# One decoder layer on one core: the order of ScalarE, VectorE, loads and TensorE in the up and down projections, from a scheduler's order to a list made in the kernel

## The chip, the core and the metric

The kernel runs on one NeuronCore of a Trainium2 chip. The metric is the time of one execution in microseconds (us) on the device. The kernel before was run three times: 1428.9, 1429.55 and 1432.31 us, so its median is 1429.55 us. One more execution was taken with the hardware profiler; that one took 1434.5 us.

## The reference, cut to what matters

One layer of a hybrid decoder: 256 tokens, width 2048, all in f32. An input projection, a state-space scan beside windowed attention and an output projection come first and are not touched. Then follows the part that the change is about, the feed-forward network, and after it a gated embedding:

```python
u = _rmsnorm(h, ffn_norm_g[i]) @ w_up[i]                    # 2048 -> 2 x 5632
u = _causal_dwconv(u, ffn_conv_w[i], ffn_conv_b[i])         # 3 taps along the tokens
g_ff, u_ff = jnp.split(u, [D_FF], axis=-1)
h = h + (jax.nn.silu(g_ff) * u_ff) @ w_down[i]              # 5632 -> 2048
gate = jax.nn.sigmoid(_rmsnorm(h, ple_norm_g[i]) @ w_ple_gate[i])
pe = _rmsnorm(p[i] @ w_ple_proj[i], ple_post_g[i])
h = h + gate * pe
```

## The kernel before, in words

**Three products for one.** Each f32 factor is split in two parts, a rounded one (names that end in `h`) and the rest (names that end in `l`). A product is three matmuls: high by high, high by low, low by high. So each weight tile `w` (128 x 1024, 512 KB, loaded by SyncE) needs a cast on ScalarE (`wh<-w`, L206) and a subtraction on VectorE (`wl<-w,wh`, L207) before TensorE can use it. "A split" below means this pair. Seven buffers hold raw tiles, and four (a fifth in this stage) hold split ones, so a cast must wait until TensorE has used up the tile that was split five before.

**The stage.** The 5632 columns are worked in 11 pairs of 512 (a chunk of `g` and the same chunk of `u`). For one pair, `up` (L1070) runs eight blocks of 256 rows of the weights. Six are plain: two weight tiles, 24 matmuls each. Two are "mixed" (`MIXED`, blocks 0 and 4; `cell_mixed`, L991): there seven products take the place of eight, on differences of weight quarters, which VectorE forms first (`ta`, `tb`, L997) and which then go through splits of their own; a half tile goes to `vh`, `vl`. A mixed block has 21 matmuls. The eight PSUM banks hold one pair's sums. After the second mixed block, VectorE combines four banks into the staged tiles `c` (L1083 to L1088), and after the last block it adds the other four (L1092).

**The turn.** `gated` (L1050) must turn these four tiles from tokens on partitions to features on partitions: ScalarE copies each into 16-bit halves (`half`, L1041), SyncE issues a DMA transpose (`flip<-half`, L1043), and ScalarE joins the halves (`uc<-flip`, L1044). Then follow the three taps (`cv<-uc`: one pass on ScalarE, two on VectorE, L308 and L310), SiLU, the product and its split into `gh`, `gl`. The taps are put in a list `later`, from which `step` issues one or two behind each block.

**The down projection** (`down`, L1112) takes two pairs at a time (`SEGS`): four output chunks, 48 matmuls each, two of them behind each `up`. Each chunk is added to the residual `h` on VectorE (L418). The first two pairs have no `down` between them, nor is there one between the second and the third.

**The way in.** Four small embedding products (`embed`, L913; their results `c` are copied by VectorE at L918 and stored to `pe_d` by SyncE at L919), the RMS factor `rh` (squares on ScalarE, a power on GpSimd), the scaled residual `cv` (`norm`, L923), and 32 transposes on TensorE with gain and split (`left`, L946; `ah<-b` L209, `al<-b` L210).

**Who sets the order.** On TensorE the order is that of the code (`tc.manual_schedule` with that engine alone). ScalarE, VectorE and SyncE are ordered by the scheduler of the framework, which simulates the program; `high_priority` lifts the squares, `rh`, and the first norms and lefts. PSUM banks come from a pool of eight that goes round. Every engine then works through its own list in order: what stands behind a waiting instruction waits too.

Of the kernel before, what the change touches and what calls it, by code (L numbers as in the profile page):

```python
# [11 lines left out]
F32 = mybir.dt.float32  # L12
F32R = mybir.dt.float32r
# [29 lines left out]
MIXED = (0, 4)  # L43
# [16 lines left out]
def _turns(value):  # L60

    t = value / (2 * PI)
    return _parts(t - round(t), 13, 26)


@with_exitstack
def hybrid_layer(
# [56 lines left out]

    def bank():
        return banks[0].tile([P, NC], F32, tag="b", name=nm("b"))
# [535 lines left out]
    with tc.tile_pool(name="att_s", bufs=2) as as_, tc.tile_pool(name="att", bufs=2, reuse_waits="tile") as ap_, tc.tile_pool(name="ps_sc", bufs=1, space=PSUM) as ps_sc:  # L662
# [224 lines left out]
    by_hand = tc.manual_schedule(engines={PE.engine})  # L887
    by_hand.__enter__()

    with tc.tile_pool(name="ffn", bufs=2, reuse_waits="tile") as fp:  # L890

        def staged(i):
            return sb(fp, [P, NC], f"c{i}", bufs=1)

        more.append(fp)

        class Gated:

            def __init__(self):
                self.t = []  # L900

            def add(self):
                self.t.append([sb(fp, [P, KG, T], f"g{e}", F32R, 3) for e in "hl"])
                return self.t[-1]

            def __call__(self, k, b):
                return [t[:, k % KG, b * P : (b + 1) * P] for t in self.t[k // KG]]

        gT = Gated()
        gT.add()  # L910
        ph, pl = em

        def embed(n):  # L913
            acc = acc_pair()
            gemm(acc, lambda k, b: (ph[:, k, b * P : (b + 1) * P], pl[:, k, b * P : (b + 1) * P]), [w_pe[n, 0]])
            for b in range(NB):
                t = staged(n % 2 * 2 + b)
                V.tensor_copy(t, acc[b])  # L918
                nc.sync.dma_start(pe_d[b, :, n * NC : (n + 1) * NC], t)  # L919

        normed = []

        def norm(n):  # L923
            t = sb(fp, [P, NB, NC], f"cv{n % 2}", bufs=1)
            for b in range(NB):
                hs = hres[b][:, n * NC : (n + 1) * NC]
                if n:
                    S.activation(out=t[:, b, :], in_=hs, func=AF.Copy, scale=rh[:, b : b + 1])
                else:
                    V.tensor_scalar_mul(t[:, b, :], hs, rh[:, b : b + 1])  # L930
            normed.append(t)
# [322 lines left out]
```

## Time and profile before

| | |
|---|---|
| Median of three runs | 1429.55 us |
| The profiled execution, its own time | 1434.5 us |
| Its span, first to last instruction | 1432.6 us |
| TensorE busy | 1413.0 us (99%), 6461 matmuls |
| VectorE busy | 1114.0 us (78%) |
| ScalarE busy | 903.0 us (63%) |
| GpSimd busy | 130.3 us (9%) |
| The stage that the change is about | about 608 to 1343 us of the span |

How to read it: matmuls overlap in the pipeline, so a record of 0.39 us starts every 0.2257 us when nothing holds TensorE up, and the "busy" time covers small delays. A better measure of a delay is the time from one matmul's start to the next, or the number of matmuls in a window of fixed length. TensorE is the engine without slack; the others matter where TensorE waits for them.

### The profile page before, as it was taken

The page shows a single profiled execution, that of the slowest core. Times are in us where ns is not written, and L with a number is a line of the kernel's source. Part 1 is how long each engine was busy: PE and PEld are TensorE (multiplying, and loading weights), DVE is VectorE, ACT ScalarE, POOL GpSimd, SP SyncE. Part 2 cuts the span into 40 slices and gives each one's busy share as a digit, 9 for nine tenths or more (in the row PEclk, how much of TensorE's full clock was granted, in tenths as well). Part 3 has the DMA queues.
Part 4 walks back from the last instruction along what each step waited for, and adds up shares of the span by engine and source line. Part 5 has one row for each costly group of instructions (what it writes and reads, how often), then busy time and mean ns, then how long its engine had stood idle before and what let it go on. Part 6 is the DMA issues. An engine that isn't in the chain of part 4 may idle for free.

```text
span 1432.6 us, 18128 instructions
## 1 busy us (share of the span) xinstructions
PE 1413.0 (99%) x6461; PEld 1154.4 (81%) x6461; DVE 1114.0 (78%) x1480; ACT 903.0 (63%) x1196; POOL 130.3 (9%) x113
## 2 busy tenths in 40 slices
PE   9999999999999999999999999999999999999998
PEld 7888888888777778878787888888888888788887
DVE  7678876776678898698998796878778797877764
ACT  6675555644667757566777476666758576674653
POOL 0002010008344332000000000000000000000000
PEclk9999999999999999999999999999999999999999
DMA  9656656548686878576678777686777777677671
GB/s 348 229 174 197 216 179 189 163 147 231 180 221 186 209 215 219 180 233 199 200 231 194 227 223 204 205 230 204 205 226 196 228 227 207 195 220 213 224 249 64
DMA packets 164906, 296.80 MB, mean 207 GB/s; under 512 B 93200, under 2 KB 96080, under 8 KB 164176
## 3 DMA queue, kind: packets, MB, share of 16 engines
q1 hardware_dynamic: 163952, 292.04, 69.1%
q10 hardware_dynamic: 864, 3.62, 0.7%
q8 instruction: 50, 0.82, 0.2%
q14 instruction: 40, 0.33, 0.1%
HBM read 270.41 MB, written 4.23 MB: 192 GB/s over the span
## 4 chain that ended last, share of the span: by engine, by line
PE 56%; DVE 7%; ACT 3%; DMA 2%; issue 2%; DVEq 0%; ACTq 0%
PE b L987 9%; PE b L988 9%; PE b L986 9%; PE b L244 7%; PE b L242 7%; PE b L243 7%; DVE wl L207 3%; PE acc L242 3%; PE acc L243 2%; PE acc L244 2%; DMA flip<-half 2%; ACT wh L206 1%; DVE cv L310 1%; ACT half L1041 1%; DVE h L418 1%
## 5 line engine op out<-in xcount | busy, mean ns | idle before, releaser
L207 DVE TENSOR_TENSOR wl<-w,wh 128x1024 fp32r<-128x1024 f32 (+1 forms) x473 | 584.0, 1242 | 224.3 <-ACT wh L206 220.7
L206 ACT CAST wh<-w 128x1024 fp32r<-128x1024 f32 (+1 forms) x473 | 490.3, 1045 | 339.3 <-PE b L988 135.9
L987 PE MATMUL b<-wl,ah 128*128 128x512 f32 x484 | 189.3, 391 | 2.8 <-DVE wl L207 2.7
L988 PE MATMUL b<-wh,al 128*128 128x512 f32 x484 | 189.4, 391 | 1.8 <-DVE al L210 1.7
L986 PE MATMUL b<-wh,ah 128*128 128x512 f32 x484 | 189.3, 391 | 1.2 <-ACT wh L206 1.2
L243 PE MATMUL acc<-wl,ah 128*128 128x512 f32 x448 | 176.8, 395 | 1.4 <-DVE wl L207 1.4
L242 PE MATMUL acc<-wh,ah 128*128 128x512 f32 x448 | 176.0, 396 | 0.7 <-DVE h L418 0.6
L244 PE MATMUL acc<-wh,al 128*128 128x512 f32 x448 | 175.6, 392 | 0.0
L242 PE MATMUL b<-wh,gh 128*128 128x512 f32 x352 | 137.1, 390 | 0.0
L244 PE MATMUL b<-wh,gl 128*128 128x512 f32 x352 | 137.0, 389 | 0.0
L243 PE MATMUL b<-wl,gh 128*128 128x512 f32 x352 | 136.9, 389 | 0.0
L987 PEld LDWEIGHTS b<-wl,ah 128*128 128x128 f32 x484 | 91.2, 188 | 23.1 <-DVE wl L207 4.4
L988 PEld LDWEIGHTS b<-wh,al 128*128 128x128 f32 x484 | 91.1, 188 | 21.8 <-DVE al L210 3.1
L986 PEld LDWEIGHTS b<-wh,ah 128*128 128x128 f32 x484 | 91.2, 188 | 20.7 <-ACT wh L206 1.6
L242 PE MATMUL acc<-wh,yh 128*128 128x512 f32 x256 | 101.2, 395 | 2.3 <-DVE nm L774 2.0
L242 PEld LDWEIGHTS acc<-wh,ah 128*128 128x128 f32 x448 | 84.1, 188 | 20.4 <-issue 1.1
L243 PEld LDWEIGHTS acc<-wl,ah 128*128 128x128 f32 x448 | 84.2, 188 | 19.9 <-DVE wl L207 2.2
L243 PE MATMUL acc<-wl,yh 128*128 128x512 f32 x256 | 99.8, 390 | 0.0
L244 PE MATMUL acc<-wh,yl 128*128 128x512 f32 x256 | 99.6, 390 | 0.0
L244 PEld LDWEIGHTS acc<-wh,al 128*128 128x128 f32 x448 | 84.2, 188 | 17.7 <-issue 0.7
L244 PEld LDWEIGHTS b<-wh,gl 128*128 128x128 f32 x352 | 66.1, 188 | 13.8
L243 PEld LDWEIGHTS b<-wl,gh 128*128 128x128 f32 x352 | 66.1, 188 | 13.7
(287 smaller groups left out, 2251.4 us busy)
## 6 DMA issues: line engine op xcount, KB each, us to landing
w<-in_w_up_dram SPq DMA_DIRECT2D x176, 512.0 KB, 4.5
w<-in_w_in_dram SPq DMA_DIRECT2D x126, 512.0 KB, 4.1
w<-in_w_down_dram SPq DMA_DIRECT2D x88, 512.0 KB, 4.4
w<-in_w_out_dram SPq DMA_DIRECT2D x64, 512.0 KB, 4.4
w<-in_w_pg_dram SPq DMA_DIRECT2D x32, 512.0 KB, 4.3
seg<-scr SPq DMA_DIRECT2D x8, 512.0 KB, 5.0
xt<-in_xT_dram SPq DMA_DIRECT2D x16, 128.0 KB, 7.1
h<-in_x_dram SPq DMA_DIRECT2D x2, 1024.0 KB, 8.8
```

What stands on the lines that cost most here:

```text
L206: S.copy(hi, src)
L207: V.tensor_tensor(out=lo, in0=src, in1=hi.bitcast(F32), op=ALU.subtract)
L242: PE.matmul(acc[b], lhsT=hi, rhs=wh[:, i, :], start=(k == 0), stop=False)
L243: PE.matmul(acc[b], lhsT=hi, rhs=wl[:, i, :], start=False, stop=False)
L244: PE.matmul(acc[b], lhsT=lo, rhs=wh[:, i, :], start=False, stop=(k == total - 1 or (b == NB - 1 and k + 1 == whole)))
L310: V.scalar_tensor_tensor(out=dst[:, s:], in0=ps[:, : T - s], scalar=taps[n - 1 - s], in1=dst[:, s:], op0=ALU.mult, op1=ALU.add)
L418: V.tensor_tensor(out=hs, in0=hs, in1=acc[b], op=ALU.add)
L986: PE.matmul(self.t[m], lhsT=hi, rhs=wh, start=m not in self.used, stop=False)
L987: PE.matmul(self.t[m], lhsT=hi, rhs=wl, start=False, stop=False)
L988: PE.matmul(self.t[m], lhsT=lo, rhs=wh, start=False, stop=not self.left[m])
L1041: S.copy(half.rearrange("p (a n) -> p a n", a=2), us[b].bitcast(U16).rearrange("p (n a) -> p a n", a=2))
```

## The change

The feed-forward stage is written again as a list of jobs. Each job names its engine, a duration (for instance 1.0 us for a cast, 1.17 us for a subtraction of a whole tile, 0.41 us for a tap, 0.2275 us for a matmul), the jobs that it follows, the buffers that it takes, and a `lag` behind its end until others may use the result (2.2 us for a load, 6.5 us for a transpose, 2.0 us for a store of `pe_d`). The jobs of TensorE keep the order of the code. `Plan.run` gives each job a latest start, counted back from TensorE's order as if TensorE never waited (`late`), then walks forward: whenever an engine is free it takes, of the jobs that are ready, the one with the earliest `late`. The calls are then issued in that order, and `manual_schedule` now covers TensorE, ScalarE, VectorE and SyncE. No time is read while the kernel runs; the outcome is a fixed order.

Besides: the mixed blocks are 1 and 5; the first pair takes the blocks in the order 0, 2, 3, 4, 6, 1, 5, 7 and the others from 0 to 7; PSUM banks are given by number; in a mixed block the matmuls of one split tile stand together in every pair. The numbers of instructions on each engine are the same as before, and their order up to the stage is the same.

```diff
-MIXED = (0, 4)
+MIXED = (1, 5)
+BEGIN = [0, 2, 3, 4, 6, 1, 5, 7]
+STEADY = [0, 1, 2, 3, 4, 5, 6, 7]
...
+class Plan:
+
+    HOP = 0.15
...
+    def run(self):
+        clock, last = 0.0, None
+        for j in self.jobs:
+            j.late, j.then = math.inf, []
+            for ring, i in j.slots:
+                if i >= ring.n:
+                    j.after.extend(ring.frees[i - ring.n])
+                elif ring.at:
+                    j.at = max(j.at, ring.at[i])
+            if j.engine == "PE":
+                j.late = clock
+                clock += j.dur
...
+        for j in reversed(order):
+            for k in j.then:
+                j.late = min(j.late, k.late - self.hop(j, k) - j.dur)
...
+            t, e = best
+            j = min((j for j in waiting[e] if j.ready <= t), key=lambda j: j.late)
+            waiting[e].remove(j)
+            j.start, end = t, t + j.dur
+            idle[e] = end
+            done.append(j)
+            for k in j.then:
+                k.ready = max(k.ready, end + self.hop(j, k))
...
+        for j in done:
+            j.fn()
...
-        with tc.high_priority():
-            squares(ssh, 3)
-
-    with tc.high_priority():
-        rh = finish_rstd(ssh, "rh")
...
-    banks.append(ctx.enter_context(tc.tile_pool(name="ps8", bufs=8, space=PSUM, reuse_waits="tile")))
+    banks.append(ctx.enter_context(tc.tile_pool(name="ps8", bufs=1, space=PSUM, reuse_waits="tile")))
...
-    by_hand = tc.manual_schedule(engines={PE.engine})
+    by_hand = tc.manual_schedule(engines={PE.engine, S.engine, V.engine, nc.sync.engine})
...
+            o.job = plan.add("SP", 2.0, go, slots=[o.slot], lag=2.2)
...
+            a = plan.add("ACT", 1.0, hi, after, [o.slot])
+            b = plan.add("DVE", 1.17, lo, [a, *after])
...
+                out_ = plan.add("SP", 0.9, lambda b=b, t=t: nc.sync.dma_start(pe_d[b, :, n * NC : (n + 1) * NC], t()), [put], lag=2.0)
...
-            ucs = [turned(us) for us in (gu, yz)]
...
-            later.extend([lambda e=e, f=f: conv(e, f) for e in range(2) for f in range(4)] + [mult])
...
+                j0 = plan.add("ACT", 1.0, halve, [made], [h.slot])
+                j1 = plan.add("SP", 1.0, flip, [j0], [f.slot], lag=6.5)
+                j2 = plan.add("ACT", 1.1, join, [j1], [slot])
...
+                        job = plan.add("DVE", 0.41, tap, [job])
...
+                q, p = (high, low) if c == 1 else (low, high)
+                up(c, (*p, *q), STEADY if c else BEGIN, None if c else before)
+                if pending:
+                    for n in range(4)[i * 4 // np_ : (i + 1) * 4 // np_]:
+                        down(pending, n, (p[:2], p[2:])[n % 2] if np_ > 1 else (p[:2], p[2:], q[:2], q[2:])[n])
...
+        plan.run()
```

Three places show what moves. The first is VectorE on the way in: `c<-b` are copies of embedding results, `al<-b` the low parts of the first block's left factor, `uc` the sums for the mixed block's left factor. Before:

```order
L918 COPY c_1142_5487<-b_5467 128x512
L207 TENSOR_TENSOR wl_5636<-w_5633,wh_5635 128x1024
L918 COPY c_1143_5490<-b_5468 128x512
L207 TENSOR_TENSOR wl_5654<-w_5651,wh_5653 128x1024
L210 SCALAR_TENSOR_TENSOR al_1146_5499<-b_5493,gains_94,ah_1145_5498 128x256
L965 TENSOR_TENSOR uc_5509<-uc_5509 128x128
L918 COPY c_1157_5543<-b_5523 128x512
L965 TENSOR_TENSOR uc_5509<-uc_5509 128x128
L918 COPY c_1158_5546<-b_5524 128x512
L210 SCALAR_TENSOR_TENSOR al_1146_5499<-b_5493,gains_94,ah_1145_5498 128x256
```

The same place now:

```order
L1112 COPY c_1149_5513<-b_5477 128x512
L1112 COPY c_1151_5521<-b_5481 128x512
L1032 TENSOR_TENSOR wl_5528<-w_5466,wh_5502 128x1024
L1181 SCALAR_TENSOR_TENSOR al_1153_5524<-b_5506,gains_94,ah_1152_5523 128x256 x2
L1032 TENSOR_TENSOR wl_5553<-w_5406,wh_5511 128x1024
L1112 COPY c_1164_5565<-b_5530 128x512
L1112 COPY c_1165_5567<-b_5534 128x512
```

Both low parts of the first block now stand ahead of the copies of the last embedding product; one split stands between the earlier copies and them, where two stood.

The second place is ScalarE at the beginning of the fourth pair: `uc<-flip` joins what a DMA transpose has brought, `wh<-ta` and `wh<-tb` are the casts of the mixed block. Before:

```order
L1044 COPY uc_6726<-flip_1419_6729 128x4x256
L206 CAST wh_6895<-w_6893 128x1024
L206 CAST wh_6932<-w_6926 128x1024
L1044 COPY uc_6726<-flip_1421_6734 128x4x256
L206 CAST wh_6942<-ta_6930 128x1024
L308 ACTIVATE cv_1442_6847<-uc_6726,fcw_144 128x256 x4
L1062 ACTIVATE cv_1427_6757<-cv_1427_6757 128x1024
L206 CAST wh_6948<-tb_6931 128x1024
```

The same pair's beginning now:

```order
L1028 CAST wh_6890<-w_6756 128x1024
L1028 CAST wh_6913<-ta_6847 128x1024
L1295 COPY half_1464_6917<-c_1430_6758 128x1024
L1303 COPY uc_6921<-flip_1451_6852 128x4x256
L1028 CAST wh_6939<-tb_6871 128x1024
L1295 COPY half_1471_6943<-c_1433_6777 128x1024
L1303 COPY uc_6921<-flip_1456_6875 128x4x256
```

The cast of `ta` stands ahead of the joins now, and one pass lies between the first join and the cast of `tb`. Only the first transposes of the pair are joined here; the last two are joined further down. Counted over the stage, at least three casts of weights stand between a `half` and its join now, and at least one before.

The third place is VectorE after a pair's product (`cv<-cv,cv`); TensorE takes the weight tiles w_8068, w_8086, w_8104, w_8122 in this order. Before:

```order
L1065 TENSOR_TENSOR cv_1655_7831<-cv_1655_7831,cv_1670_7921 128x1024
L207 TENSOR_TENSOR wl_8071<-w_8068,wh_8070 128x1024
L207 TENSOR_TENSOR wl_8107<-w_8104,wh_8106 128x1024
L997 TENSOR_TENSOR ta_8162<-w_8160,w_8158 128x512
L997 TENSOR_TENSOR ta_8162<-w_8160 128x512
L207 TENSOR_TENSOR wl_8125<-w_8122,wh_8124 128x1024
L207 TENSOR_TENSOR gl_7454<-cv_1655_7831,gh_7453 128x1024
L207 TENSOR_TENSOR wl_8089<-w_8086,wh_8088 128x1024
```

A pair's product now, where TensorE takes w_8085, w_8102, w_8123, w_8146 in this order:

```order
L1351 TENSOR_TENSOR cv_1689_7962<-cv_1689_7962,cv_1724_8121 128x1024
L1032 TENSOR_TENSOR wl_8214<-tb_8143,wh_8210 128x1024
L1360 TENSOR_TENSOR gl_8232<-cv_1689_7962,gh_8216 128x1024
L1032 TENSOR_TENSOR wl_8234<-w_8085,wh_8230 128x1024
L1032 TENSOR_TENSOR wl_8246<-w_8102,wh_8242 128x1024
L1032 TENSOR_TENSOR wl_8263<-w_8123,wh_8251 128x1024
L1032 TENSOR_TENSOR wl_8275<-w_8146,wh_8271 128x1024
```

Before, the split that TensorE takes second came fourth, behind two splits, two subtractions and `gl`; now the splits stand in TensorE's order.

More of the change, by code (lines that the diff above doesn't have):

```diff
@@ new lines, in multiply, with pick, piece @@
+        def multiply(parts, after):
+            slots = [s for bank_, _, _ in parts for s in bank_.open()]
+            calls = [bank_.product(left, right) for bank_, left, right in parts]
+            job = on_pe(calls, after, slots, 3 * UNIT * len(calls))
+            for bank_, _, _ in parts:
+                bank_.last = job
+            return job
+        def pick(o, i):
+            return lambda: (o.h[:, i, :], o.l[:, i, :])
+        def piece(o, i, b):
+            return lambda: (o.h[:, i, b * P : (b + 1) * P], o.l[:, i, b * P : (b + 1) * P])
@@ new lines, in square, with go @@
+        def square(ss, n, b, after=(), at=-20.0):
+            def go():
+                sq = sb(small, [P, NC], "hsq")
+                S.activation(out=sq, in_=hres[b][:, n * NC : (n + 1) * NC], func=AF.Square, accum_out=ss[:, b, n : n + 1])
+            return plan.add("ACT", 0.72, go, after, at=at)
+        rh = []
+        sq = [square(ssh, 3, b, at=1.2 + 0.6 * b) for b in range(NB)]
+        rh_job = plan.add("DVE", 0.3, lambda: rh.append(finish_rstd(ssh, "rh")), sq, lag=1.9)
+        normed = [norm(n, rh_job) for n in range(KG)]
@@ new lines, in hybrid_layer, with turn, before @@
+        low, high = (0, 1, 2, 3), (4, 5, 6, 7)
+        embed(0, (4, 5))
+        embed(1, (6, 7))
+        embed(2, (0, 1))
+        turned_in = []
+        def turn(n):
+            for kp in sorted((2 * n, 2 * n + 1), key=lambda kp: kp in MIXED):
+                left(kp, normed[n], 4 + kp % 4)
+            turned_in.append(n)
+        turn(0)
+        embed(3, (2, 3))
+        def before(n):
+            for m in range(KG):
+                if m not in turned_in and m <= max(BEGIN[: n + 2]) // 2:
+                    turn(m)
@@ L1137, in hybrid_layer @@
-        h2T = Lhs(act, KT, "a")
-        def after(n):
-            squares(ssg, n)
-            if n:
-                next_lhs(h2T, n - 1, g_ple)
-        down(pending, range(4), after)
-    more.pop()
+        for np_ in SEGS:
+            for i in range(np_):
+                c = pair + i
+                q, p = (high, low) if c == 1 else (low, high)
[3 more added lines that the diff above has]
+                        down(pending, n, (p[:2], p[2:])[n % 2] if np_ > 1 else (p[:2], p[2:], q[:2], q[2:])[n])
+            pending = (pair, np_)
+            pair += np_
@@ new lines, in hybrid_layer @@
+        ssg = sb(small, [P, NB, 4], "ssg", bufs=1)
+        was = None
+        for n in range(4):
+            jobs = down(pending, n, ((4, 5), (6, 7), (0, 1), (2, 3))[n])
+            for b in range(NB):
+                square(ssg, n, b, [jobs[b]])
+            if n:
+                turn_h(n - 1, ((4, 5), (6, 7))[(n - 1) % 2], was)
+            was = jobs
+        plan.run()
+        h2T = h2T[0]
+    by_hand.__exit__(None, None, None)
+    by_hand = tc.manual_schedule(engines={PE.engine})
```

570 lines of the change are left out of this document (384 added, 186 removed).

## The prediction

> **What bounds the kernel now.** The page comes first: which engine has no slack.
>
> ```profile
> span 1432.6 us, 18128 instructions
> PE 1413.0 (99%) x6461; PEld 1154.4 (81%) x6461; DVE 1114.0 (78%) x1480; ACT 903.0 (63%) x1196; POOL 130.3 (9%) x113
> ```
>
> TensorE (PE) is idle for 19.6 us of the span. An order changes no work on it, so the change can win no more than what TensorE loses in the stage. Second, windows of 100 us show where it loses: the number behind PE's busy time is the matmuls that started.
>
> ```profile
> 700.00:800.00 100.00, 97.92 (x421) 80.00 (x422) 88.95 (x116) 69.56 (x80) 0.00 (x0) 0.98 0.78 221
> 800.00:900.00 100.00, 100.00 (x443) 82.84 (x442) 79.19 (x102) 66.91 (x75) 0.00 (x0) 1.00 0.76 220
> 900.00:1000.00 100.00, 99.45 (x440) 82.04 (x439) 83.56 (x104) 63.90 (x72) 0.00 (x0) 1.00 0.69 204
> ...
> 1200.00:1300.00 100.00, 98.60 (x436) 81.34 (x435) 79.83 (x105) 69.02 (x78) 0.00 (x0) 1.00 0.73 209
> sum 700.00, PE 693.25 PEld 571.20 DVE 580.95 ACT 472.10 POOL 1.61; mean PE 99.03 PEld 81.60 DVE 82.99 ACT 67.44 POOL 0.23
> ```
>
> An undisturbed window holds 443 matmuls, one per 0.2257 us, at the full granted clock (1.00); that is the floor. VectorE (DVE), 79 to 89% busy, is next, but not full. The list of waits says who holds TensorE up in the stage:
>
> ```profile
> PE b L987 <- DVE wl L207: 3.7, 4, 1.4
> PE b L988 <- DVE al L210: 1.7, 2, 0.9
> PE b L986 <- ACT wh L206: 1.2, 1, 1.2
> ```
>
> Seven waits, six of them for VectorE, for splits of weights or of the left factor. They show only the time after TensorE ran dry, so I price each from the timeline of TensorE, start to start.
>
> ```profile
> 620.65 0.40 PE L987 MATMUL b<-wl,ah 128*128 128x512 f32 x1
> ...
> 623.16 0.50 PE L988 MATMUL b<-wh,al 128*128 128x512 f32 x1 [0.75 <-DVE al L210]
> ...
> 629.45 0.39 PE L987 MATMUL b<-wl,ah 128*128 128x512 f32 x1
> 630.77 0.50 PE L988 MATMUL b<-wh,al 128*128 128x512 f32 x1 [0.93 <-DVE al L210]
> ...
> 698.68 0.39 PE L986 MATMUL b<-wh,ph 128*128 128x512 f32 x1
> 699.99 0.50 PE L987 MATMUL b<-wl,ph 128*128 128x512 f32 x1 [0.93 <-DVE wl L207]
> ```
>
> From 620.65 to 623.16 there are four steps from one start to the next, three matmuls standing in between: 2.51 us for 0.90, a loss of 1.61. The second costs 1.32 less 0.23, 1.09 us, the third 1.08 us. The fourth is the largest; two windows of 10 us hold it:
>
> ```profile
> 770.00:780.00 10.00, 7.92 (x33) 5.73 (x32) 8.11 (x14) 7.52 (x10) 0.00 (x0) 1.00 0.52 175
> 780.00:790.00 10.00, 10.00 (x38) 8.06 (x38) 10.00 (x12) 6.25 (x8) 0.00 (x0) 0.83 0.53 165
> ```
>
> At 44.3 matmuls per 10 us they lack 11.3 and 6.3, together 17.6, which is 4.0 us (the 100 us window lacks 22, 5.0 us: the upper bound). The second window's loss is not waiting: the granted clock was 0.83 there. Windows 900 to 1000 and 1200 to 1300 lack 3 and 7 matmuls, 0.7 and 1.6 us. The stage loses 1.6 + 1.1 + 1.1 + 4.0 + 0.7 + 1.6 = 10.1 us, at most 11.1.
>
> **The change part by part.**
>
> *The low parts of the first block* (first stretch, 1.6 and 1.1 us).
>
> ```profile
> 617.16 0.69 DVE L918 COPY c<-b 128x512 f32<-128x512 f32 x1 [1.62 <-DMA pe_d<-c]
> 617.77 1.22 DVE L207 TENSOR_TENSOR wl<-w,wh 128x1024 fp32r<-128x1024 f32 x1
> ...
> 620.63 0.48 DVE L210 SCALAR_TENSOR_TENSOR al<-b,gains,ah 128x256 fp32r<-128x256 f32 x1
> DMA to landing us min/median/max: 3.6/5.4/9.8
> ```
>
> (The last row is the view of `pe_d`: issue to landing.) VectorE waits at a copy until an earlier copy's store has landed, and the block's `al` stand behind it; the second comes after 622, and TensorE waits. In the new order both `al` stand behind two copies and one split. The wait itself stays: the list reckons 0.9 + 2.0 = 2.9 us for the store, the trace has 5.4. With VectorE held to 617.16 as now, the two copies take 1.2 us (a copy ends 0.61 us behind its start, by the row that follows it), the split 1.15, and each `al` 0.4: they are ready by 619.9 and 620.3. The first block's third matmul comes at about 620.8 and needs the first of them; the second is needed at 621.5. Margin 0.9 us: the 1.6 us go. If the store lands at its slowest, 9.8 us, 4.4 us later, TensorE waits 3.5 us. The next block's `al` follow one split, two copies, one split, so 620.3 + 1.15 + 1.2 + 1.15 + 0.8, at 624.6, for a block that begins 5.4 us behind 620.34: the 1.1 us go too.
>
> *The fourth pair* (4.0 us): three engines, one chain.
>
> ```profile
> 763.93 2.23 SPq L1043 DMA_TRANSPOSE flip<-half  x1
> 772.48 1.17 ACT L1044 COPY uc<-flip 128x1024 uint16<-128x1024 uint16 x1 [2.69 <-DMA flip<-half]
> 773.56 1.04 ACT L206 CAST wh<-ta 128x1024 fp32r<-128x1024 f32 x1
> 774.63 1.23 DVE L207 TENSOR_TENSOR wl<-ta,wh 128x1024 fp32r<-128x1024 f32 x1 [1.89 <-ACT wh L206]
> 775.78 2.84 DVE L310 SCALAR_TENSOR_TENSOR cv<-uc,fcw,cv 128x255 f32<-128x255 f32 x7
> 778.54 1.22 DVE L207 TENSOR_TENSOR wl<-tb,wh 128x1024 fp32r<-128x1024 f32 x1
> ```
>
> A transpose landed 8.5 us behind its issue. ScalarE stood 2.69 us at the join, with the cast of `ta` behind it, though nothing about `ta` hangs on the join. VectorE then put seven taps, 2.84 us, ahead of the last split. In the new order the cast of `ta` precedes the joins, the taps follow both splits, and a plain block of 24 matmuls (5.4 us) comes before the mixed one. The joins have more cover as well: at least three casts of weights behind their `half`, which in a plain stretch is three times 12 matmuls, 8.1 us, against one before. The list reckons 7.5 us from a transpose's start to its use; the trace has
>
> ```profile
> DMA to landing us min/median/max: 2.7/5.1/8.5
> ```
>
> so the reckoning covers all but the slowest. What is late next there is the cast of `tb` behind one join, with the plain block's 5.4 us ahead of it. I take the whole 2.6 us of waiting as won.
>
> The other part is the clock: 0.17 of 10 us were not granted, the 780 window's 6.3 missing matmuls, 1.4 us. It follows these waits directly, and it is the only loss of clock in the windows above, so I take it to go with them. [...]
>
> *Splits out of turn* (0.7 and 1.6 us).
>
> ```profile
> 915.85 1.22 DVE L207 TENSOR_TENSOR gl<-cv,gh 128x1024 fp32r<-128x1024 f32 x1
> 916.99 1.22 DVE L207 TENSOR_TENSOR wl<-w,wh 128x1024 fp32r<-128x1024 f32 x1
> ```
>
> The last of these is a split that TensorE needs before the ones that stand ahead of `gl`. The old order has such an inversion in seven places, and in two of them the late split stands behind two later ones: the shape of these rows, which comes again in the 1200 window. The new order has none in 514 splits, so both go.
>
> *The third pair* (1.1 us at 699): here VectorE has little slack. For a pair, TensorE does 6 x 24 + 2 x 21 = 186 matmuls, 42 us. VectorE does 18 splits at 1.15 (774.63 to the next row's start), 18 half-tile passes (subtractions, `vl`, sums) at 0.6, 16 taps at 0.4 (2.84 us for seven), product and `gl` at 1.15: 40 us. Only where a `down` follows (96 matmuls, 21.7 us, for 11.6 us of VectorE) is there room. The list may defer the taps until that `down` needs them and takes splits by deadline, so I count the 1.1 us as won, with a lower bound of nothing.
>
> *Banks, block order, queues.* Matmuls, casts and passes are as many as before. In the fixed scheme a mixed block's four banks are those the previous pair freed early or the last `down` used, a plain block (5.4 us) earlier: four additions of 0.6 us fit. Moving later `pe_d` stores behind nine loads on SyncE costs nothing: their tiles are written next by the first pair's sums, some 30 us on. At the end of the stage the last `down` products, squares and transposes keep their sequence, and the first gate splits stand no later than before: nothing.
>
> **The sum.** 10.1 us go; I leave 0.5 us for small waits that the list did not price (the 0.9 us margin above): 1434.5 - 9.6 = 1424.9 us on the profiled execution's own basis (its span is 1432.6, with 1.9 around it). But that execution lies 4.95 us above the median of 1429.55. Work on TensorE does not vary, so the difference is waiting, and the question is which. Of TensorE's 19.6 us idle, 6.75 (700 less 693.25) lie in the windows from 600 to 1300, and 12.9 outside them, the beginning and the end of the span among these; so I put half, 2.5 us, in the stage. Then an ordinary run loses 7.6 us there, 7.1 are won, and the median becomes 1429.55 - 7.1 = 1422.5 us. If all of the 4.95 lies in the stage (the late transpose alone is 4.0), it becomes 1424.9; if none, 1419.9.
>
> **The rivals.**
>
> *The stalls only move* (0.22). The list is fixed, and stores and transposes land when they will; at the first block alone a slow store takes back 3.5 us, and one transpose at the join before `tb` 1 to 3 us. For it: the list's 2.9 us for a store that takes 5.4. Against: margins otherwise of a cast or more. Taking back 5 of the 7.1 us leaves 1427.5, between 1426 and 1430.
>
> *Slower: loads for the mixed blocks* (0.10). VectorE's `ta` waits for the second raw tile of the block, and everything behind it waits too.
>
> ```profile
> DVE ta L997 <- DMA w<-in_w_up_dram: 12.1, 11, 2.7
> w<-in_w_up_dram SPq DMA_DIRECT2D x176, 512.0 KB, 4.5
> ```
>
> Eleven of 22 waited, 1.1 us each, without stopping TensorE. In the new order the buffer for this tile comes free two splits (2.3 us of VectorE's work) before `ta`, and the load needs 4.5: up to 2.2 us of waiting, 22 times. While TensorE paces the splits (one per 2.7 us) it is hidden; in the pairs where VectorE is at 40 of 42 us it is not. If 0.7 us of each reaches TensorE, 22 x 0.7 = 15 us come back, against 7.1 won: 1437.5. It decides from 0.32 us each.
>
> *The clock is lost all the same* (0.06), for a cause other than the waits: 1422.5 + 1.4 = 1423.9. Against it speaks that no other window has lost any. [...]
>
> **How the numbers follow.** The forecast, stalls gone, has 0.62 and its own range is 1419.9 to 1424.9. With the moved stalls the range must reach up: 1417 to 1430 leaves out the slower case, the tail above 1430 and little below. A measurement of this kernel can tell 0.3%, 4.3 us, from no change: faster means below 1425.3. The forecast gives 0.57 to faster, the clock rival 0.05, the moved stalls 0.04; the same gets 0.25, slower 0.09.
>
> **What would show it.** In the changed profile: 443 matmuls in every 100 us window from 700 to 1300, with a clock of 1.00; no wait for `al` between 620 and 632; no wait for `wh` or `wl` at the fourth pair's start; VectorE still stopping at the copy of the third embedding. Wrong would be: waits of TensorE that recur once a pair with `ta` waiting for a load just before (the slower rival), a half clock without waits ahead of it, or full windows with an unchanged median, which would mean that ordinary runs never had these stalls.

## The result, and the profile after

The changed kernel took 1422.42 us (median of 6 runs, 1419.79 to 1425.02), the kernel before 1429.22 us in the same comparison (6 runs, 1426.0 to 1434.0). The ratio is 0.9948 with a 95% interval of 0.9924 to 0.9972: 6.8 us won. The profiled execution took 1419.79 us.

The head of the page shows the idle time of TensorE halved: 1418.1 less 1407.6 is 10.5 us, against 19.6 before.

```profile
span 1418.1 us, 18146 instructions
PE 1407.6 (99%) x6461; PEld 1153.4 (81%) x6461; DVE 1116.9 (79%) x1480; ACT 906.7 (64%) x1196; POOL 128.5 (9%) x113
```

The windows of the changed kernel; behind PE's busy time stands the number of matmuls that ran in the window, and near the row's end the granted clock. One that runs across an edge is counted on both sides, so an undisturbed window of 100 us shows 443 where some 441 start, one every 0.2267 us; the 0.2257 us ahead of the prediction and in it are 100 us by 443. Differences between windows are not touched by this.

```profile
400.00:500.00 100.00, 99.94 (x492) 78.19 (x490) 83.31 (x101) 71.96 (x137) 44.12 (x35) 1.00 0.79 213
...
600.00:700.00 100.00, 100.00 (x459) 83.09 (x458) 86.07 (x115) 70.56 (x95) 0.71 (x1) 1.00 0.75 227
700.00:800.00 100.00, 100.00 (x443) 82.81 (x442) 94.31 (x129) 77.73 (x89) 0.00 (x0) 1.00 0.73 215
...
1200.00:1300.00 100.00, 100.00 (x443) 82.80 (x442) 81.78 (x104) 67.89 (x76) 0.00 (x0) 1.00 0.74 218
```

Two windows of before that the prediction did not show:

```profile
400.00:500.00 100.00, 97.72 (x478) 75.40 (x477) 82.76 (x99) 71.85 (x137) 41.76 (x35) 1.00 0.81 208
...
600.00:700.00 100.00, 97.27 (x441) 79.30 (x439) 86.49 (x124) 73.25 (x98) 1.61 (x1) 1.00 0.68 205
```

From 700 to 1300 every window of after holds 443 matmuls (one 442), and 600 to 700 holds 459 against 441 before. Call 459 and six times 443, 3117, the full stage. After has 3116 of them, before 3067: 50 matmuls are missing there, 11.3 us at 0.2257 us each, and 1 is missing in after. TensorE has no wait in the stage at all in this execution. The window from 400 to 500 is ahead of the stage, where the order of instructions is the same in both kernels. It won 14 matmuls as well (3.2 us at the same rate), and the 2821st matmul, ahead of the stage in both, starts at 596.2 us instead of 599.3. That is no work of the change; it is how much one execution differs from another. So 14.7 us between the two profiled executions and 6.8 between the medians do not contradict each other.

What the prediction asked of VectorE and ScalarE can be read from two timelines of after. On VectorE, on the way in (`c<-b` copies of the embedding products, `al` the first block's low parts):

```profile
607.35 1.28 DVE L1112 COPY c<-b 128x512 f32<-128x512 f32 x2
...
612.80 1.29 DVE L1112 COPY c<-b 128x512 f32<-128x512 f32 x2
...
615.13 0.87 DVE L1181 SCALAR_TENSOR_TENSOR al<-b,gains,ah 128x256 fp32r<-128x256 f32 x2
```

The low parts are done at 616.0; the first matmul that takes one, the third of the first block, starts at 617.69. VectorE did not stop at the third product's copies (612.80), because the first stores had landed. The first copies come at 607.35 instead of 610.91, but 3.2 of these 3.6 us are the lead that this execution had already; against TensorE they moved 0.4 us. What changed is the time that the stores took. Before, SyncE had issued five loads just ahead of the first two stores, and the stores took 5.4 us to land:

```profile
602.11 9.24 SPq L215 DMA_DIRECT2D w<-in_w_up_dram  x5
611.62 0.99 SPq L919 DMA_DIRECT2D pe_d<-c  x2
```
```profile
DMA to landing us min/median/max: 5.4/5.4/5.4
```

In the list no load stands just ahead of them, and they took 2.6 and 3.3 us:

```profile
608.06 0.93 SPq L1114 DMA_DIRECT2D pe_d<-c  x2
609.08 0.41 SPq L319 DMA_DIRECT2D w<-in_w_up_dram  x1
```
```profile
DMA to landing us min/median/max: 2.6/3.0/3.3
```

On ScalarE, at the beginning of the fourth pair:

```profile
764.83 1.05 ACT L1028 CAST wh<-ta 128x1024 fp32r<-128x1024 f32 x1 [1.67 <-DVE wl L1032]
765.78 1.04 ACT L1295 COPY half<-c 128x1024 uint16<-128x1024 uint16 x1
766.73 1.17 ACT L1303 COPY uc<-flip 128x1024 uint16<-128x1024 uint16 x1
767.80 1.05 ACT L1028 CAST wh<-tb 128x1024 fp32r<-128x1024 f32 x1
```

The cast of `ta` waits for no transpose. Its low part is done at 767.14, 7.6 us ahead of the matmul that takes it first (774.78); before, it was done at 775.86 and the matmul that needed it started right behind, at 775.91. VectorE's taps follow at 772.99, behind the splits of `ta` and `tb` (768.88). What VectorE waits for at the `ta` differences, the sign of the slower rival, shrank from 12.1 us in 11 waits:

```profile
DVE ta L1234 <- DMA w<-in_w_up_dram: 3.8, 6, 1.9
```

### The profile page after: what moved, and what is told of

Same layout as the page of the kernel before. It is cut to its first block, busy times and chain, and to the rows that moved or that the text cites. A ratio compares the mean times of both kernels' runs of the same rounds, so it can differ in the third digit from the quotient of the medians.

```text
span 1418.1 us, 18146 instructions
## 1 busy us (share of the span) xinstructions
PE 1407.6 (99%) x6461; PEld 1153.4 (81%) x6461; DVE 1116.9 (79%) x1480; ACT 906.7 (64%) x1196; POOL 128.5 (9%) x113
## 4 chain that ended last, share of the span: by engine, by line
PE 92%; issue 3%; DVE 3%; ACT 1%; DMA 0%; POOL 0%; DVEq 0%; SPq 0%; POOLq 0%; ACTq 0%
PE b L1074 17%; PE b L1076 17%; PE b L1075 17%; PE acc L346 10%; PE acc L347 10%; PE acc L348 10%; PE b L346 2%; PE b L348 2%; PE b L347 2%; DVE wl L311 1%; PE acc L455 1%; PE ms L663 1%; PE sc L866 1%; PE tr L907 0%; PE tr L425 0%
## 5 line engine op out<-in xcount | busy, mean ns | idle before, releaser
L311 DVE TENSOR_TENSOR wl<-w,wh 128x1024 fp32r<-128x1024 f32 (+1 forms) x227 | 288.8, 1280 | 125.0 <-ACT wh L310 119.9
L1032 DVE TENSOR_TENSOR wl<-w,wh 128x1024 fp32r<-128x1024 f32 x246 | 299.9, 1222 | 98.4 <-ACT wh L1028 97.0
L1028 ACT CAST wh<-w 128x1024 fp32r<-128x1024 f32 x246 | 258.7, 1053 | 167.3 <-PE b L1076 127.7
L310 ACT CAST wh<-w 128x1024 fp32r<-128x1024 f32 (+1 forms) x227 | 233.7, 1037 | 175.6 <-PE acc L348 99.0
L1076 PE MATMUL b<-wh,al 128*128 128x512 f32 x500 | 194.6, 389 | 0.0
L1076 PEld LDWEIGHTS b<-wh,al 128*128 128x128 f32 x500 | 93.8, 188 | 19.6
```

The source lines that it names most:

```text
L310: S.copy(hi, src)
L311: V.tensor_tensor(out=lo, in0=src, in1=hi.bitcast(F32), op=ALU.subtract)
L1028: S.copy(o.h, src.t)
L1032: V.tensor_tensor(out=o.l, in0=src.t, in1=o.h.bitcast(F32), op=ALU.subtract)
L1076: PE.matmul(t, lhsT=lo, rhs=wh, start=False, stop=last)
```

## The experiments

Each kernel is one of the two with one thing changed. The last column counts the matmuls that are missing from 3117 between 600 and 1300 us, times 0.2257 us, in the one profiled execution. The ratios are to the kernel before.

| Kernel | Median us | Ratio (95% interval) | Lost in the stage, us |
|---|---|---|---|
| changed | 1422.42 | 0.9948 (0.9924 to 0.9972) | 0.2 |
| ScalarE, VectorE, SyncE by the scheduler | 1426.04 | 0.9972 (0.9961 to 0.9983) | 4.7 |
| list in code order | 1429.8 | 1.0005 (0.9995 to 1.0016) | 8.1 |
| code order, taps last | 1423.65 | 0.9959 (0.9945 to 0.9973) | 1.6 |
| deadlines, taps first | 1424.53 | 0.9965 (0.995 to 0.9979) | 2.9 |
| mixed blocks first | 1422.96 | 0.996 (0.9947 to 0.9974) | 1.1 |
| transposes reckoned at 2.0 us | 1421.43 | 0.9946 (0.9932 to 0.9961) | 0 |
| the way in put back | 1423.73 | 0.9958 (0.9941 to 0.9974) | 1.8 |
| before, with priorities | 1431.92 | 1.0012 (0.9999 to 1.0025) | 11.1 |
| changed, turn on ScalarE | 1434.58 | 1.0036 (1.0021 to 1.0051) | 0 |

**Is it the order on the other engines, or blocks and banks?** The changed kernel, with the scheduler back on three engines:

```diff
-    by_hand = tc.manual_schedule(engines={PE.engine, S.engine, V.engine, nc.sync.engine})
+    by_hand = tc.manual_schedule(engines={PE.engine})
```

> Everything of the change stays (blocks, banks, the list, and the calls in the list's order), but ScalarE, VectorE and SyncE are ordered by the framework's scheduler again; only TensorE's order is by hand. Theory A (the gain comes from the order on ScalarE and VectorE: low parts, joins and splits that stood in the wrong place): waits of TensorE for al, wl or wh come back in the stage, 3 to 8 us of lost matmul starts, time 1425 to 1430 us. Theory B (the gain comes from the new places of the mixed blocks and from banks by number, which leave every engine more room, so that the order on the other engines is of little account): no more than 1 us of waits in the stage, time within 2 us of 1422.4.

About half of the gain went (1426.04), by theory A. Nearly all that is missing (19 of 21 matmuls) is in the window from 700 to 800, at the third and the fourth pair. Its waits of TensorE, and one of ScalarE that the changed kernel does not have:

```profile
PE b L1075 <- DVE wl L1032: 1.7, 3, 0.8
PE b L1074 <- DVE c L1281: 0.8, 1, 0.8
```
```profile
ACT uc L1303 <- DMA flip<-half: 15.9, 12, 3.5
```

The way in stayed won (458 of 459 matmuls), although VectorE did stop at the third product's copy for 0.40 us (617.38): both low parts, behind two copies and one split, were done by 620.64, and the matmuls that take them start on time, at 620.89 and 621.57.

So half of the gain does not need the order by hand. What the half that stays comes from (the blocks, the banks, or the calls in the list's order, which the scheduler also sees) no run separates. The next run has the same blocks and banks and wins nothing, so these alone are not enough; SyncE's order was not tested apart from the other two.

**Is it the deadline, or any fixed order with true durations?** The same list, walked by the order of the code:

```diff
-            j = min((j for j in waiting[e] if j.ready <= t), key=lambda j: j.late)
+            j = min((j for j in waiting[e] if j.ready <= t), key=self.jobs.index)
```

> The list is walked with the same durations and lags, but of the jobs that are ready an engine takes the one that was written first, not the one with the earliest latest start. Theory A: the deadline is what defers taps, products and gl behind the splits; without it a pair's sixteen taps (0.4 us each, 6.6 us together) and its product go ahead of splits, and where no down projection follows VectorE has 2 us of slack in 42: TensorE waits at the three pairs' starts without a down projection before and, less, at others, 3 to 8 us, 1425 to 1430 us. Theory B: a fixed order with true durations is enough, splits are three to four tiles ahead (8 to 11 us), so the taps fit: within 2 us of 1422.4, no wait in the stage.

Theory A, and the whole gain is gone: 1429.8 us, no difference from before. VectorE at the fourth pair shows the same picture as before the change:

```profile
773.33 1.22 DVE L1032 TENSOR_TENSOR wl<-ta,wh 128x1024 fp32r<-128x1024 f32 x1
774.47 0.69 DVE L1234 TENSOR_TENSOR tb<-w,ta 128x512 f32<-128x512 f32 x1
775.07 3.74 DVE L1338 SCALAR_TENSOR_TENSOR cv<-uc,fcw,cv 128x255 f32<-128x255 f32 x8
778.85 1.23 DVE L1351 TENSOR_TENSOR cv<-cv,cv 128x1024 f32<-128x1024 f32 x1
779.99 0.69 DVE L1234 TENSOR_TENSOR tb<-w,tb 128x512 f32<-128x512 f32 x1
780.59 1.22 DVE L1032 TENSOR_TENSOR wl<-w,wh 128x1024 fp32r<-128x1024 f32 x1
781.72 1.22 DVE L1360 TENSOR_TENSOR gl<-cv,gh 128x1024 fp32r<-128x1024 f32 x1
```

Eight taps and a product, 4.9 us, stand between the two halves of `tb`, and TensorE ran dry. No join waited for a transpose here, so the taps and the product are enough. This was tested from both sides. Code order, but with taps, product and `gl` taken only when nothing else is ready:

```diff
-            j = min((j for j in waiting[e] if j.ready <= t), key=lambda j: j.late)
+            j = min((j for j in waiting[e] if j.ready <= t), key=lambda j: (j in self.taps, self.jobs.index(j)))
...
```

> The reverse: the list goes by the order in which the jobs were written, as in the run by code order, only that taps, a pair's product and the subtraction behind it are taken when nothing else is ready. Theory J: this alone gives back most of the 7.4 us that the code order lost, 1422 to 1425 us. Theory K: it gives back less than half, 1426 us or more, with waits for ta, tb or the left factor's sums in other places.

And the deadlines, but with taps and product taken as soon as one is ready:

```diff
-            j = min((j for j in waiting[e] if j.ready <= t), key=lambda j: j.late)
+            j = min((j for j in waiting[e] if j.ready <= t), key=lambda j: (j not in self.taps, j.late))
...
```

> The list goes by latest start as in the changed kernel, but VectorE takes a tap or a pair's product whenever one is ready, ahead of all else. Theory J (the deferral of the taps is what the deadline is worth: eight taps and a product, 4.9 us in one piece, stood ahead of a tb and its split in the run by code order): TensorE waits for wl at the third and fourth pair again, 4 to 8 us, 1426 to 1430 us. Theory K (the deadline works through all the jobs: joins, halves and casts on ScalarE stay by deadline here, so the taps are ready late and in small groups, and what follows them is placed around them): 0 to 2 us of waits, 1422 to 1424 us.

Putting the taps last gave back 6.2 of the 7.4 us (theory J). Putting them first lost only 2.1 us (nearer to K than to the 4 to 8 us of J), in one wait of 1.69 us at 714, where again eight taps and a product (701.15 to 706.1) stood ahead of `ta`. My reading is that ScalarE's joins, still by deadline, keep most taps from being ready early; no run took that alone away. Among these lists the place of taps, product and `gl` is most of what the deadline is worth.

**Is the cover needed that the prediction named?** It named two: a plain block ahead of the mixed one, and 7.5 us from a transpose's start to its use.

```diff
-STEADY = [0, 1, 2, 3, 4, 5, 6, 7]
+STEADY = [1, 0, 2, 3, 5, 4, 6, 7]
```

> The mixed blocks go first and fifth again from the second pair on, as before the change (the order of blocks is 1, 0, 2, 3, 5, 4, 6, 7; the first pair is left as it is); all else is by the list, which is made anew for it. Theory A' (the plain block ahead of the mixed one is the cover that the prediction named: 5.4 us): without it the sums of the last down projection (0.6 us each), the subtractions ta and tb and two more splits stand right behind one another, TensorE waits 0.5 to 1.5 us at most pairs' starts, 4 to 10 us together, 1426 to 1432 us. Theory A (only the order within ScalarE and VectorE counts, the deadlines find it for this block order as well): no wait over 0.3 us in the stage, within 2 us of 1422.4.

```diff
-                j1 = plan.add("SP", 1.0, flip, [j0], [f.slot], lag=6.5)
+                j1 = plan.add("SP", 1.0, flip, [j0], [f.slot], lag=2.0)
```

> The list reckons 2.0 us instead of 6.5 from a transpose's issue to its use, so a join may stand 3 to 4 us before its data are there (5.1 us median, 8.5 at most from issue to landing). Theory A (a join that waits holds the casts behind it): ScalarE waits at a good part of the 44 joins, 1 to 3 us each, 30 to 60 us together; splits are about three tiles ahead, so most of it stays hidden and TensorE loses 1 to 5 us at a few pairs: 1423 to 1427 us. Theory C (the margin in the list is of no account, since only a transpose that is late by several us, once in 44, reaches TensorE): ScalarE waits the same, TensorE nothing, within 1 us of 1422.4.

Neither is needed, each taken away by itself. With the mixed blocks first from the second pair on, one wait of 0.6 us is all that TensorE has in the stage: theory A by the time, though it allowed no wait over 0.3 us. With the short reckoning ScalarE waits at the joins (and 6.7 us more before a `half`, put down to a transpose too), far less than expected, and TensorE nowhere (theory C):

```profile
ACT uc L1303 <- DMA flip<-half: 8.3, 9, 1.6
```

The scheduler's version above waited 15.9 us at joins, and 3.5 us in one. Waits up to 1.6 us did not reach TensorE: they lay inside the lead of the splits.

**Was the profiled execution of before an ordinary one?** The same kernel, profiled again:

> The kernel before once more, for a second trace. Theory A with the prediction's split: an ordinary run loses about 7.6 us in the stage; at the first blocks, at 699 and at the two inverted splits the same waits stand within 0.5 us, and the fourth pair's 4.0 us are less or gone, as the transpose there took 8.5 us, the slowest of 44. Theory D (the stalls belong to one run): other places, or less than 4 us in the stage.

It took 1427.73 us. Its windows:

```profile
600.00:700.00 100.00, 97.49 (x441) 79.47 (x440) 87.58 (x125) 73.51 (x98) 1.61 (x1) 1.00 0.66 205
700.00:800.00 100.00, 99.74 (x439) 81.89 (x438) 90.43 (x118) 71.63 (x83) 0.00 (x0) 1.00 0.78 228
...
1200.00:1300.00 100.00, 99.56 (x440) 82.12 (x439) 80.98 (x105) 67.73 (x77) 0.00 (x0) 1.00 0.75 214
```

26 matmuls are missing, 5.9 us. The first stretch lacks 18, as in the first trace; the fourth pair nearly nothing (4, with the clock at 1.00) against 22; the stall at 1237 lost 0.6 us against 1.6, the one at 917 less than 0.3. Theory A in the main, the same places with the late transpose gone; only the stall at 1237 shrank by 1.0 us, where 0.5 was allowed. At the fourth pair the order is the same as in the first trace, the seven taps ahead of the last split with it. But the join waited 0.73 us instead of 2.69:

```profile
768.96 1.17 ACT L1044 COPY uc<-flip 128x1024 uint16<-128x1024 uint16 x1 [0.73 <-DMA flip<-half]
772.26 2.85 DVE L310 SCALAR_TENSOR_TENSOR cv<-uc,fcw,cv 128x255 f32<-128x255 f32 x7
776.30 0.50 PE L987 MATMUL b<-wl,ah 128*128 128x512 f32 x1 [0.26 <-DVE wl L207]
```

The taps alone thus cost at most 0.9 us there in this order; with the late transpose, and the half clock that followed, it was 5.0.

**The way in by itself.** Four conditions put the old order back there:

```diff
...
+        for j in copies[:2]:
+            j.after.append(plan.lows[5])
+        parts[0].after.append(plan.lows[7])
+        parts[1].after.append(copies[7])
```

> Only the way in is put back, by four extra conditions in the list: the first embedding product's two copies behind two splits that now follow them (about 3 us later), the first low part of the first block behind one more split, the second behind the last embedding product's copies. Theory A (the prediction's account of the first 1.6 us): VectorE stops at a copy of the third product until a store has landed, the low parts come after the first block has begun, and TensorE loses 1 to 3 us between 617 and 632, nothing later in the stage; time 1423.5 to 1425.5 us. Theory D (in an ordinary run the stores land in time, so that this stall was one of the profiled run alone): no wait for al, time within 1 us of 1422.4.

The time, 1423.73 us, tells too little by itself; the trace shows 8 matmuls missing, 1.8 us, all in the first window. VectorE stops for stores again:

```profile
621.53 0.48 DVE L1185 SCALAR_TENSOR_TENSOR al<-b,gains,ah 128x256 fp32r<-128x256 f32 x1
622.75 0.69 DVE L1115 COPY c<-b 128x512 f32<-128x512 f32 x1 [0.74 <-DMA pe_d<-c]
624.35 0.69 DVE L1115 COPY c<-b 128x512 f32<-128x512 f32 x1 [0.91 <-DMA pe_d<-c]
```

The wait of TensorE (0.9 us at 623.49) is put down to a copy, which frees a bank, not to `al`. The first block's low parts were done at 620.5 and 622.0, in time for the matmuls at 621.36 and 622.06. So the loss lies where theory A has it, and a late store behind which VectorE stops does cost TensorE time; that the low parts cost it, as in the kernel before, this run doesn't show.

**What does an inversion cost?** The subtraction of one weight tile was put behind that of the tile 1, 2, 3 or 4 places later, twice each:

```diff
...
+        for at, by in zip(plan.places[::2], (1, 2, 3, 3, 4, 4, 2, 1)):
+            plan.lows[at].after.append(plan.lows[at + by])
```

> In eight of the down projections the subtraction of the third weight tile is put behind the subtraction of the tile one, two, three, three, four, four, two and one places later; nothing else is changed, but the list is made anew with these conditions. Theory E (the prediction's reading: the place is what costs; one place nothing, two places 0.7 to 1.6 us): waits for wl of 0.7 to 1.6 us at the two inversions by two, more at three and four. Theory F (an inversion costs only what exceeds the lead of the splits: with five split buffers the subtraction three places on can be done 1.0 + 1.15 us after a buffer comes free, 2.7 us before the late tile is needed): nothing at one and two places, 0.3 to 1 us at three, 3 to 4 us at four, and the two stalls of the kernel before came from what else stood there (ta, tb, gl). In the sum by E 5 to 8 us and by F 7 to 10 us above 1422.

All of TensorE's waits in the stage, in order of time, are those of three, three, four and four places:

```profile
882.30 0.50 PE L1076 MATMUL b<-wl,gh 128*128 128x512 f32 x1 [0.63 <-DVE wl L1032]
...
947.14 0.50 PE L1076 MATMUL b<-wl,gh 128*128 128x512 f32 x1 [0.64 <-DVE wl L1032]
...
1014.72 0.56 PE L1076 MATMUL b<-wl,gh 128*128 128x512 f32 x1 [3.35 <-DVE wl L1032]
...
1083.85 0.79 PE L1076 MATMUL b<-wl,gh 128*128 128x512 f32 x1 [3.35 <-DVE wl L1032]
```

Start to start 0.8 and 3.5 us are lost; one and two places cost nothing. Theory F holds in size, theory E falls. The one execution took 1434.3 us: 8.6 us of stalls, and 1.7 us of half clock behind each of the two long ones (the granted clock was 0.83 from 1010 to 1020 us and from 1080 to 1090; around the first stall of 0.8 us it was 1.00).

**Which stall costs the clock?** ScalarE reads a PSUM bank 2 to 9 times between two weight tiles, so that TensorE stands still once. This kernel leaves out the sums of the first two weight tiles for one bank in those eight chunks, so it doesn't compute the layer:

```diff
...
+                if s == 1 and count:
+                    for _ in range(count):
+                        held = [plan.add("ACT", 0.6, lambda: S.copy(sb(small, [P, NC], "hsq"), pair_[0]()), held)]
```

> In eight down projections ScalarE reads a PSUM bank 2, 3, 4, 5, 6, 7, 8 and 9 times between the second and the third weight tile, so that TensorE stands still once in each, for about 0.6 us times the reads less 0.4 (0.8 to 5.0 us, an estimate from the 0.6 us of a half-tile pass). The sums of the first two weight tiles are left out for one bank in those eight chunks. The question is which stall costs the clock. Theory G (the stalls before the clock loss at 780 us caused it; they were 2.4 us of idle time with one matmul between): half clock of some 3.4 us follows every stall from 2.4 us on, so the last five, 1.7 us each. [...] Theory I (stalls have nothing to do with it): no loss behind any of the eight. The time is 20 us or more above 1422 in each case.

The eight stalls, start to start, lost 0.6, 1.1, 1.6, 2.1, 2.6, 3.1, 3.6 and 4.1 us. Windows of 10 us around the last five:

```profile
945.00:955.00 10.00, 8.05 (x36) 6.32 (x35) 5.44 (x7) 7.47 (x12) 0.00 (x0) 1.00 0.80 197
1015.00:1025.00 10.00, 7.55 (x26) 5.71 (x26) 5.82 (x9) 8.64 (x13) 0.00 (x0) 0.83 0.54 180
1083.00:1093.00 10.00, 7.07 (x25) 5.34 (x24) 5.34 (x8) 8.81 (x13) 0.00 (x0) 0.83 0.60 190
1152.00:1162.00 10.00, 6.58 (x17) 4.84 (x16) 4.47 (x7) 7.76 (x13) 0.00 (x0) 0.66 0.58 171
1222.00:1232.00 10.00, 6.09 (x21) 4.57 (x20) 4.95 (x7) 8.59 (x14) 0.00 (x0) 0.83 0.63 172
```

The window with the stall of 2.1 us kept a clock of 1.00; those with 2.6, 3.1 and 4.1 us show 0.83, which is 3.4 us at half speed, and the one with 3.6 us shows 0.66, twice that. Theory G, with four such stalls instead of five, as each was shorter than expected. In the time, 1450.05 us in one execution, the stalls make 18.9 us and the five pieces of half clock in these windows, with one more from 500 to 600 us (0.98 of 100 us), ahead of the stage, 1.7 each, 10 us: 29 us against the 28 above 1422.

**Two attempts at more.** The kernel before, with high priority for the loads and splits of the blocks and of `down`:

```diff
+                with tc.high_priority():
+                    (cell_mixed if kp in MIXED else cell_plain)(acc, kp, c)
...
```

> The kernel before, with one thing added: the loads, casts, subtractions and weight differences of the blocks, and the loads and splits of the down projection, are given high priority in the framework's scheduler. Theory J: the splits go ahead of taps, the waits at the third and fourth pair and the two late splits go, the way in stays (1 to 2.5 us): 1424 to 1426 us. Theory L (the scheduler's model of the time is what puts things in the wrong place, not the missing deadline): the places shift, no gain, 1427 to 1431 us.

No gain (1431.92; the interval of the ratio is 0.9999 to 1.0025): theory L, 0.9 us above its range. VectorE's timeline where TensorE lost 2.1 us, from 1233.60:

```profile
1227.81 1.22 DVE L1065 TENSOR_TENSOR cv<-cv,cv 128x1024 f32<-128x1024 f32 x1
1228.95 2.35 DVE L207 TENSOR_TENSOR wl<-w,wh 128x1024 fp32r<-128x1024 f32 x2
1231.22 0.69 DVE L997 TENSOR_TENSOR ta<-w,w 128x512 f32<-128x512 f32 x1
...
1233.56 1.22 DVE L207 TENSOR_TENSOR gl<-cv,gh 128x1024 fp32r<-128x1024 f32 x1
1234.69 1.22 DVE L207 TENSOR_TENSOR wl<-w,wh 128x1024 fp32r<-128x1024 f32 x1
```

The priority left product, `ta` and `gl` ahead of the split that was wanted. The other attempt went at what is left ahead of the stage:

```diff
+            copy = S.copy if n > NC else G.tensor_copy
-            G.tensor_copy(dst.bitcast(U16).rearrange("p c (t a) -> p c t a", a=2), flip.rearrange("p (a c) t -> p c t a", a=2))
+            copy(dst.bitcast(U16).rearrange("p c (t a) -> p c t a", a=2), flip.rearrange("p (a c) t -> p c t a", a=2))
```

> The changed kernel, and ahead of the stage the twelve copies that follow the transposes of the attention weights go from GpSimd to ScalarE. In the changed kernel's trace a split on VectorE took 3.16 us instead of 1.22 while GpSimd copied 128x2048 beside it, and TensorE then lost 1.9 us at 500 us, 1.4 at 369. Theory M (the two engines' collision is what is left to win): splits of 2 to 3 us go, 1 to 3 us are won, 1419.5 to 1421.5 us. Theory N (ScalarE, in order, now waits for the transposes with casts behind it, as in the joins of the kernel before): TensorE waits for wh instead, 0 to 6 us slower, 1422 to 1428 us.

(The edit takes the two copies of the keys along.) It lost 12 us, theory N and twice its size:

```profile
ACT s L818 <- DMA flip<-half: 35.3, 10, 6.8
```

ScalarE stands 35 us before ten transposes, with casts behind it, and 9.7 us before the two of the keys. It is the stall at a join, as in the kernel before, in another stage. The granted clock was 0.98 from 300 to 400 us and 0.97 from 500 to 600, which makes about 5 of the 12 us.

## Why the prediction was right

**The time.** 1422.5 was forecast and 1422.42 measured; 7.1 us were to be won, 6.8 were. The sum for the profiled execution, 10.1 us and at most 11.1, stands against 50 missing matmuls, 11.3 us. The window from 700 to 800 is where it was low: 22 matmuls, 5.0 us, where 4.0 went into the sum. The two windows of 10 us were held against 44.3 matmuls; but an undisturbed one shows 45 or 46, as those at its edges count, so some 21 were missing and not 17.6. The choice to lay half of that execution's excess into the stage gave an ordinary loss of 7.6 us; the second trace of before has 5.9. The two traces of before differ by 6.6 us, and 5.7 of these lie in the stage (from the starts of the 2821st and the 5901st matmul), which speaks for a larger share than half. So that the forecast came within 0.1 us of the median is luck: the sum was too small, the share probably too, and the two errors work against each other. Both of the forecast's bounds, 1419.9 and 1424.9, lie inside the interval that the ratio leaves (1418.4 to 1425.2).

**The way in.** The outcome was right, the margin not by the reason given. "The wait itself stays" is the sentence that failed. It gave the store the 5.4 us of the trace before, but the list also moved the loads away from it, and the first store landed in 2.6 us, inside the 2.9 that the list reckons. So VectorE did not stop. Where it still did, in the run with the scheduler back, the reckoning held: two copies, a split and both low parts took 3.3 us from the stop's end, where 3.1 were reckoned, and TensorE lost nothing. The slow store of 9.8 us, from which the rival of the moved stalls takes its 3.5 us, was misread: that view holds two loads of `pe` at the kernel's end as well, and the eight stores alone took 3.6 to 6.1 us. Putting the old order back brought 1.8 of the 2.7 us, by another link.

**The fourth pair.** The cast of `ta` ahead of the join and the taps behind the splits were the right things to name; both have been seen apart. With the taps in code order TensorE ran dry without a late transpose; in the kernel before, the same taps with a transpose in time cost at most 0.9 of the 5.0 us. The taps used up the lead, and the late transpose then reached TensorE. The two covers named beside them (the plain block, the 7.5 us) were not needed.

**The clock.** It went with the waits, as taken; by the record of the granted clock it cost 1.7 us (3.413 us at half speed), where 1.4 went into the sum. Ahead of it stood stalls of 1.3 and 1.1 us with one matmul between (from 776.95 us), and in the run with the stalls by ScalarE, above, half clock followed one of 2.6 us. The rival in which the clock is lost for another cause does not show: every window of after from 600 to 1300 us has a clock of 1.00.

**Splits out of turn.** Both stalls went, but the place two behind is not their cause, as the prediction had it. Two places cost nothing by themselves; what stood there besides, a product, two subtractions and `gl` (about 3.5 us), made them late. That the stalls shrank from 0.7 and 1.6 us to under 0.3 and 0.6 in the second trace fits this: they hang on how far VectorE lags. That part is argued; no run took only the product away. (The 514 splits of the prediction are nearly all of the kernel's 517; the stage has 290.)

**The third pair** was counted as won and was; the 0.5 us kept for small waits were not needed. Neither the slower rival (3.8 us of waits for raw tiles, none passed on) nor the moved stalls show in the changed kernel's trace.

## What to carry to other kernels

On an engine that works its list in order, what counts is not how early each piece can run but which piece is wanted first downstream: sort by latest start, and give work with slack the gaps. True durations alone, walked in the order of the code, won nothing; the deferral of one group of cheap passes won most. The order of the loads counts too: here a small store behind them took twice as long (5.4 us against 2.6), and VectorE waited 1.6 us for its buffer. Before pricing an operation out of turn, count the lead of the buffers between the engines: inside it an inversion is free, beyond it each place costs a whole step (0.8 us at three places here, 3.5 at four).

## What the runs showed of the hardware

**The clock.** In the trace of the kernel before the granted clock fell to half once ahead of the last microsecond: it was 1.00 from 776.95 to 780.12 us, 0.50 from there to 783.53 and 1.00 again behind. The piece of 3.413 us cost 1.7 us. TensorE had lost 2.4 us just ahead of it, in two stalls. What came behind other losses, by the mean granted clock of the stretch around each:

| Run, us from the span's start | TensorE lost, us | Granted clock |
|---|---|---|
| inversions, 880 to 890 | 0.8 | 1.00 |
| before, 1200 to 1300 | 1.6 | 1.00 |
| stalls by ScalarE, 945 to 955 | 2.1 | 1.00 |
| stalls by ScalarE, 1015 to 1025 | 2.6 | 0.83 |
| inversions, 1010 to 1020 and 1080 to 1090 | 3.5 | 0.83 |
| stalls by ScalarE, 1152 to 1162 | 3.6 | 0.66 |
| stalls by ScalarE, 1222 to 1232 | 4.1 | 0.83 |

Each single stall of 2.6 us or more in this table was followed by half clock, and none up to 2.1 us was. For losses in several pieces the sum alone does not say it: 2.4 us in the kernel before were followed by half clock, but in the list in code order the window from 690 to 700 us lacks 12 matmuls, 2.7 us, and it and the next show 1.00. What decides between these two cases no run shows.

**A store beside loads.** In the trace of the kernel before, three loads of 512 KB were still on their way when the first store of 256 KB was issued (611.62 us), and it took 5.4 us to land. In the changed kernel's none was (608.06 us), and it took 2.6 us. In all four executions where the scheduler orders SyncE VectorE waited for a store in the stage (0.4 to 2.3 us); of the ten with a list, only in the one with the way in put back (1.7 us). No run moved the loads alone.

**A split beside GpSimd.** Ahead of the stage a split on VectorE took 3.16 us instead of 1.22, in the same microseconds as a copy on GpSimd:

```profile
498.11 3.16 DVE L311 TENSOR_TENSOR wl<-w,wh 128x1024 fp32r<-128x1024 f32 x1
```
```profile
497.58 2.60 POOL L817 COPY s<-flip 128x2048 uint16<-128x2048 uint16 x1
```

Of the copy 2.08 us were left when the split began, and these and 1.08 us make its time. In the traces of the two kernels all 27 whole splits that began with more than 0.15 us of a GpSimd copy to come took the rest of the copy and 1.07 to 1.09 us; none of 926 beside which GpSimd did nothing took over 1.23. With the copies moved to ScalarE, above, the longest split outside the stage took 2.12 us, against 3.19 in the changed kernel. Behind the split at 498 us TensorE lost 1.9 us (499.88 to 502.01 from start to start), the largest single loss left in the changed kernel's trace.
